# Side sums of a decoder trunk set at other ticks, w_out's sums in another stage, and a buffer of its own for raw gates

## The chip, the cores and the metric

The kernel runs on one core of a Trainium2 chip. The metric is the device time of one execution in microseconds (us). Five engines work side by side, each through its own queue in order: PE (matmuls), DVE (vector), ACT (scalar, activations), POOL (GpSimd) and SP, which here issues nearly all DMAs. A profiled execution gives a trace of every instruction.

## The reference, cut to what matters

One layer (`DEPTH = 1`), batch 1, 2048 rows of 1024 channels, all in float32:

```python
mod = silu(c) @ w_ada + b_ada
shift, scale, gate = split(mod, 3)
u = x * (1.0 + scale) + shift
h = u @ w_in
q, k, v, a_gate, p_in, p_gate, m_a, m_p = split(h)
a = sliding_window_sink_attention(q, k, v, sinks, bias, mask) * silu(a_gate)
a = a @ w_attn_proj
p = einsum('bsgc,gcd->bsgd', multiscale_causal_pool(p_in), w_pool_mix)
p = (p * pool_scale) * silu(p_gate)
p = p @ w_pool_proj
y = sigmoid(m_a) * a + sigmoid(m_p) * p
y = (y @ w_out) * (1.0 + gate)
x = layer_norm(ALPHA * x + y, ln_gain, ln_bias)
```

The attention has 16 query heads of 64 channels over 2 key heads, a window of 128, and one sink for each head. The pool means run over 2, 4, 8 and 16 rows.

## The kernel before, in words

**Products.** Each float32 operand is split into a rounded high half and a low half (`act.copy`, then the subtraction `low`), and a product takes three matmuls (`mm3`). On top of that, two output tiles by two column blocks are computed with seven block products in place of eight, from sums and differences of the blocks, as in Strassen's scheme: the weights' side is the class `Quad` (four blocks in the tile `W`, one in `A22`; `sum1`, `mid` and `late` make its sums on POOL), and the other side is seven sets, `B11`, `T1`, `T2`, `B21`, `T3`, `B22`, `T4`. A product is 12 matmuls of 128x512.

**Side sums.** The sets of one stage are made out of data of an earlier one. `sums_to` does it for one pair of row blocks: it takes two `spare` rooms, loads the four blocks (`fetch`), may multiply them (`work`), subtracts in place on POOL to get `T1`, `T2`, `T4` and `T3`, and puts each result in DRAM by SP (`put`). Its list of (offset, step) is laid over the ticks of a stage that computes something else. Four stores are filled: `u1` (the modulated x of the second half), `ain` and `pin` (attention's and pool's results, one for each half `s`), and `wo` (w_out times 1 + gate). Later a stage loads a set from its store (`set_steps`) and splits it on ACT and DVE.

**Ticks.** `ring` runs groups of two quads. After each product it calls `tick`, which emits the hooks of that place; a full group has 14 ticks. What is emitted at a tick goes to the end of its engine's queue, and `defer` holds a store back by some ticks.

**Stages.** A sequence of 2048 rows goes in two halves:

- the head, then `first_phase`: gates, keys and values of the first half, beside it the `u1` sums;
- `attention` of the first half. Its steps of scores, softmax and values are interleaved with fills, products for queries (`q`), pool inputs (`mix`) and raw gates (`ma`, `mp`). `split` prepares a fill's block three products ahead: ACT copies the high half, POOL subtracts the low half. `take_gate` copies a raw gate off PSUM into a tile and stores it; `pool_sums` and `take_p` make the pool's result in the tile `fin` (ACT copies, POOL adds, DVE scales, POOL multiplies by the gate) and store it two or three steps later (`keep_raw`);
- `second_phase`: first one group of the last gates (`post`, 14 ticks), then five groups for the second half. Beside it run the sums of `wo` (four) and of the first half's `ain` and `pin` (eight). `ph.turns["spare"]` lends rooms: two of its own pool (`None`), the four query tiles `kq`, and two of the key tile `k`, all free at that time; from group 3 on, only its own pool's four are lent;
- `attention` of the second half;
- the mix: one group of the last gates, then for each half two groups of attention projection (`attn_quad`) and two of pool projection (`pool_quad`, which adds on POOL and stores `y`), then four groups with w_out and the layer norm. Beside the first groups run the sums of the second half's `ain` and `pin`.

SP's queue holds loads and stores in one order: where a store waits for the engine that makes its data, the loads behind it wait too.

Of the kernel before, what the change touches and what calls it, by code (L numbers as in the profile page):

```python
# [12 lines left out]
F32 = mybir.dt.float32  # L13
# [6 lines left out]
P = 128  # L20
# [3 lines left out]
CH = 512  # L24
# [3 lines left out]
HD = 64  # L28
# [31 lines left out]
def kernel(  # L60
# [22 lines left out]
    nc = tc.nc  # L83
# [34 lines left out]
    wo_d = set_store("wo")  # L118
# [11 lines left out]
    def low(engine, dst, src, hi):  # L130
        engine.tensor_tensor(dst, src, as32(hi), ALU.subtract)  # L131
# [63 lines left out]
    def put(q, store, name, i, src):  # L195
        q.dma_start(store[name][i // 2, :, i % 2, :], src)

    def sums_to(ph, store, i, load, work=None):

        b = []  # L200

        def x(r, c):
            return b[r][:, c * CH : (c + 1) * CH]

        def fetch():
            b.extend((ph.spare(), ph.spare()))
            b.reverse()
            for r in (1, 0):
                load(b[r], r)

        def sub(out, a, c):
            return lambda: pool.tensor_tensor(x(*out), x(*a), x(*c), ALU.subtract)

        todo = [(0, fetch)]
        if work:
            todo += [(3, lambda: work(b[0], 0)), (3.5, lambda: work(b[1], 1))]
        todo += [(at, sub(*z)) for at, z in (
            (7.5, ((0, 1), (0, 1), (0, 0))),
            (9, ((1, 1), (1, 1), (0, 1))),
            (10.5, ((1, 0), (1, 0), (1, 1))),  # L220
            (12, ((0, 0), (1, 1), (0, 0))),
        )]
        made = ((4, "B11", (0, 0)), (5, "B21", (1, 0)), (6, "B22", (1, 1))) if work else ()
        for at, name, z in (
            *made, (8.6, "T1", (0, 1)), (10.1, "T2", (1, 1)), (11.6, "T4", (1, 0)), (13.1, "T3", (0, 0)),
        ):
            todo.append((at, lambda name=name, z=z: put(sp, store, name, i, x(*z))))
        return sorted(todo, key=lambda t: t[0])

# [500 lines left out]
    def attention(ph, s, fills, post, opened):  # L730
        tp = ph.t
# [82 lines left out]
        def take_gate(name, m, t, src, kept):  # L814
            x = src
            if not kept:
                x = tp.tile([P, CH], F32, tag="fin", bufs=2, name="raw")
                act.copy(x, src)
            later(now_n[0], lambda: sp.dma_start(gates_d[name][s, m, t], x))

# [23 lines left out]
        def split(i):  # L844
            x, name = seq[i]
            q = quads[x]
            if name == "B11" and x > 1:
                q.sum1(pool)
            w = ph.split()
            hi, lo = made[i] = w[:, 0:CH], w[:, CH:]  # L850
            act.copy(hi, q.block(name))
            low(pool, lo, q.block(name), hi)
            if name == "T1":
                q.mid(pool)
            elif name == "B21":
                q.late(pool)
# [95 lines left out]
        for n in range(N + 3):  # L952
# [11 lines left out]
            if n - 3 in pvs:  # L964
                pv = pvs.pop(n - 3)
                jj, tt, bb = (n - 3) // U, (n - 3) // NB % 2, (n - 3) % NB
                if bb == 0:
                    outs[jj, tt] = tp.tile([P, CH], F32, tag="o", bufs=2, name="o")
                if bb == 1:
                    ags[jj, tt] = ld("ag", gates_d["ag"][s, jj, tt], 1)  # L970
                o2 = tp.tile([HD, 2, P], F32, tag="o2", bufs=2, name="o2")
                dve.tensor_copy(o2, pv[HD:])
                for h in range(2):
                    dve.tensor_tensor(
                        outs[jj, tt][h * HD : (h + 1) * HD, bb * P : (bb + 1) * P], pv[0:HD, h, :], o2[:, h, :], ALU.add
                    )
# [376 lines left out]
    def second_phase(ph, opened, post, plan1):  # L1353
        groups, fills, _, turn = plan1
        cb = ph.t.tile([P, D], F32, tag="cb", bufs=1, name="cb")
        hooks = {}

        def gate_rows():
            nc.scalar.dma_start(gate_d.rearrange("k p -> p k"), mod[:, 16:24], allow_slow_non_contiguous=True)
            nc.scalar.dma_start(cb, gate_d.rearrange("k p -> (k p)").partition_broadcast(P))  # L1360

        def load_wo(x, k):
            for n in range(2):
                sp.dma_start(cols(x, n), wout[k, n])

        side = []
        for i in range(4):
            ks = (i, 4 + i)
            side.append(sums_to(
                ph,  # L1370
                wo_d,
                i,
                lambda x, r, ks=ks: load_wo(x, ks[r]),
                lambda x, r: dve.tensor_tensor(x, x, cb, ALU.mult),
            ))
        for raw in (ain_d[0], pin_d[0]):
            for i in range(4):
                side.append(sums_to(ph, raw, i, load_raw(raw, i)))
        ahead, hooks = hooks, {}
        for start, todo in zip((3, 8, 12, 16, 20, 24, 28, 32, 36, 40, 57, 62), side):  # L1380
            for offset, f in todo:
                at = int(start + offset) - 14
                if at < 0:
                    ahead.setdefault((0, at + 14), []).append(f)
                else:
                    hooks.setdefault((at // 14, at % 14), []).append(f)
        later_hooks, hooks = hooks, ahead
        hooks.setdefault((0, 2), []).append(gate_rows)
        planned(hooks, ph, u1_d, True)
        opened = ring(ph, [post], opened, hooks, groups[0], lambda tick: [front(ph, q, tick) for q in groups[0]])  # L1390
        hooks = later_hooks
        planned(hooks, ph, None, False)
        hooks.setdefault((3, 0), []).append(lambda: ph.turns.clear())
        turned(hooks, lambda i: turn(ph, i), 4)
        opened_by = [q for _, _, q in fills[:2]]
        return ring(ph, groups, opened, hooks, opened_by, lambda tick: [front(ph, opened_by[0], tick)])
# [24 lines left out]
    def cols2(t, n):  # L1421
        return t[:, n * D : (n + 1) * D]
# [18 lines left out]
        opened = attention(ph, 0, plans[0][1], plans[0][2], opened)  # L1441
    with Pools("g1", spare=4, p=2, c=5) as ph:
        kq, k, v = rooms_of("second")
        ph.turns["spare"] = cycle([None, None, *kq, cols2(k, 0), cols2(k, 1)])
        opened = second_phase(ph, opened, plans[0][2], plans[1])
    with Pools("a1") as ph:
        opened = attention(ph, 1, plans[1][1], plans[1][2], opened)
# [3 lines left out]
    with Pools("mix", spare=4, p=2, c=8) as ph:  # L1451
        for k in range(4, KT):
            ta[k] = wide(ph, k)
        phases = [([plans[1][2]], None)]
        for s in range(2):
            phases.append((pairs(lambda m, s=s: attn_quad(s, m)), ain_d[s]))
            phases.append((pairs(lambda m, s=s: pool_quad(s, m)), pin_d[s]))
        outs = [out_quad(k) for k in range(0, S // P, 2)]
        phases.append(([outs[i : i + 2] for i in range(0, 8, 2)], wo_d))
        every = [(i, gi) for i, (groups, _) in enumerate(phases) for gi in range(len(groups))]  # L1460
        sides = [{} for _ in phases]
        for n, (raw, i) in enumerate((raw, i) for raw in (ain_d[1], pin_d[1]) for i in range(4)):
            for offset, f in sums_to(ph, raw, i, load_raw(raw, i)):
                at = int(2 + 7.5 * n + offset)
                i, gi = every[at // 14]
                sides[i].setdefault((gi, at % 14), []).append(f)
        for i, (groups, store) in enumerate(phases):
            hooks = sides[i]
            if i:
                planned(hooks, ph, store, False)  # L1470
            after, nxt = None, []
            if i + 1 < len(phases):
                planned(hooks, ph, phases[i + 1][1], True)
                nxt = phases[i + 1][0][0]
                after = lambda tick, nxt=nxt: [front(ph, q, tick) for q in nxt]
            else:
                for at, row in ((1, 2), (1, 3), (5, 4), (5, 5)):
                    hooks.setdefault((0, at), []).append(lambda row=row: load_z(ph, row))
            if i in (3, 5):
                ta.clear()  # L1480
            if i == 4:

                def vectors():
                    for name, src in (("gain", gain), ("lnb", lnb)):
                        vec[name] = wide(ph, len(vec))
                        sp.dma_start(vec[name], src.partition_broadcast(P))

                hooks.setdefault((-1, 5), []).append(vectors)
                hooks.setdefault((-1, 7), []).append(lambda: [load_z(ph, row) for row in range(2)])
            opened = ring(ph, groups, opened, hooks, nxt, after, i == 5)  # L1490
# [53 lines left out]
```

## Time and profile before

| | us |
|---|---|
| median of 3 runs | 1759.96 |
| the runs | 1758.97, 1759.96, 1761.0 |
| the profiled execution, its own time | 1762.15 |
| its span in the trace | 1760.3 |

The span has 24568 instructions. In the profile, lines of code are named L and their number; most operations go through a helper that records them all at line 56, so a group is told by its tile, written out<-in. `w_set` is a pair of halves of weights, `set_B...` and `set_T...` are sets, `mm` and `lg` are PSUM banks, `spare`, `second_qs` and `second_kk` are rooms of side sums, `raw` and `fin` the tiles of the attention, `g` a gate's tile in the mix.

A row of a window gives its stretch, its length, and for PE, PE's weight loads, DVE, ACT and POOL the busy time with the number of instructions in brackets, then the granted PE clock as a share of full speed, the DMA engines' mean busy share and GB/s. A row of waits gives who waited for whom: us in total, times, longest. A row of the timeline gives start, length, engine, line, operation, tiles and count, and in square brackets the engine's idle time before it and what ended that. A row of a tile's or line's own view gives minimum, median and maximum in ns, and the first and last start. In a row of groups, the busy time and the mean in ns of one follow the first bar.

In the trace, the first attention lies from about 275 to 620 us, the second projection stage from about 630 to 860, the second attention up to about 1225, and the mix from there to the end.

### The profile page before, as it was taken

How to read it: one execution, taken by the hardware profiler on the slowest of the kernel's cores; microseconds unless marked ns; L12 is line 12 of the kernel's file. 1: busy time of each engine (PE TensorE's matmuls, PEld its weight loads, DVE VectorE, ACT ScalarE, POOL GpSimd, SP SyncE). 2: the span in 40 equal slices, each digit the busy share in tenths (PEclk: the TensorE clock that was granted, in tenths of full speed). 3: DMA queues.
4: the chain of work that ended last, by engine and by line, in shares of the span. 5: the costliest groups of instructions: out<-in, count | busy, mean ns of one | idle time of the engine just before them, and what ended most of it. 6: DMA issues, size and time to landing. Idle time of an engine off the chain costs nothing.

```text
span 1760.3 us, 24568 instructions
## 1 busy us (share of the span) xinstructions
PE 1673.0 (95%) x8056; PEld 1396.0 (79%) x8056; DVE 1219.1 (69%) x2228; ACT 964.7 (55%) x2002; POOL 1087.6 (62%) x810
## 2 busy tenths in 40 slices
PE   6899999999999997999999999989999979999997
PEld 5688888888788786788788887878877758887885
DVE  5966655787667668555477786766778476869777
ACT  4544546667567554334467676765655145534552
POOL 2154337686867836894486978597576872467442
PEclk9999999999999999999999999999999999999998
DMA  9478843333423368984432434233988786677442
GB/s 347 137 286 301 219 155 96 115 126 108 138 97 102 126 240 296 318 297 140 154 120 85 138 125 134 94 92 122 347 298 295 243 288 206 225 267 259 146 143 107
DMA packets 185840, 331.54 MB, mean 188 GB/s; under 512 B 17888, under 2 KB 43632, under 8 KB 185712
## 3 DMA queue, kind: packets, MB, share of 16 engines
q1 hardware_dynamic: 182592, 325.72, 54.4%
q10 hardware_dynamic: 3088, 4.23, 1.0%
q8 instruction: 64, 1.05, 0.2%
q14 instruction: 64, 0.52, 0.1%
q0 software_dynamic: 32, 0.02, 0.0%
HBM read 223.77 MB, written 109.28 MB: 189 GB/s over the span
## 4 chain that ended last, share of the span: by engine, by line
PE 42%; POOL 8%; DVE 7%; DMA 5%; issue 4%; ACT 3%; SPq 0%; POOLq 0%; DVEq 0%; ACTq 0%
PE mm L56 27%; PE lg L56 12%; PE pv L56 2%; DVE w_set L131 2%; PE pt L56 1%; POOL spare L56 1%; POOL w_set L56 1%; POOL wide L597 1%; DMA set_T<-ain_T 1%; DVE set_T L56 1%; POOL W L256 1%; DMA W<-in_wpp_dram 1%; POOL fin L56 1%; DMA g<-mp_d 1%; DVE set_B L56 1%
## 5 line engine op out<-in xcount | busy, mean ns | idle before, releaser
L56 PE MATMUL mm<-set_B,w_set 128*128 128x512 f32 x2664 | 665.0, 397 | 21.9 <-DVE set_B L56 9.2
L56 PEld LDWEIGHTS mm<-set_B,w_set 128*128 128x128 f32 x2664 | 501.8, 191 | 134.1 <-DVE w_set L131 11.4
L56 PE MATMUL mm<-set_T,w_set 128*128 128x512 f32 x1824 | 457.8, 397 | 7.2 <-POOL w_set L56 4.1
L56 PE MATMUL lg<-set_T,w_set 128*128 128x512 f32 x1728 | 422.6, 395 | 18.3 <-DVE w_set L131 9.2
L56 PEld LDWEIGHTS mm<-set_T,w_set 128*128 128x128 f32 x1824 | 337.3, 189 | 79.4 <-POOL w_set L56 6.3
L56 PEld LDWEIGHTS lg<-set_T,w_set 128*128 128x128 f32 x1728 | 325.6, 190 | 93.5 <-DVE w_set L131 14.5
L131 DVE TENSOR_TENSOR w_set<-W,w_set 128x1024 fp32r<-128x1024 f32 x138 | 200.0, 1451 | 193.6 <-ACT w_set L293 184.6
L293 ACT CAST w_set<-W 128x1024 fp32r<-128x1024 f32 x138 | 144.8, 1050 | 268.4 <-PE mm L56 139.5
L56 POOL TENSOR_TENSOR w_set<-W,w_set 128x512 fp32r<-128x512 f32 x160 | 208.0, 1307 | 128.1 <-ACT w_set L56 122.6
L256 POOL TENSOR_TENSOR W<-W,A 128x512 f32<-128x512 f32 x46 | 67.8, 1475 | 247.0 <-DMA A<-in_win_dram 97.6
L56 ACT ACTIVATE L<-L,nm 128x257 f32<-128x257 f32 (+1 forms) x256 | 127.1, 498 | 21.9 <-DVE nm L56 15.6
L265 POOL TENSOR_TENSOR W<-W 128x512 f32<-128x512 f32 x46 | 73.1, 1589 | 99.4 <-DVE w_set L131 88.2
L56 DVE COPY o<-pv 64x256 f32<-64x256 f32 x128 | 54.2, 424 | 104.9 <-PE pv L56 103.8
L56 DVE CUSTOM_DVE_ANT_0 L<-lg,bt,nsink 128x256 f32<-128x256 f32 (+1 forms) x256 | 111.7, 473 | 21.0 <-PE lg L56 7.5
L56 ACT CAST w_set<-W 128x512 fp32r<-128x512 f32 (+1 forms) x164 | 100.2, 626 | 39.7 <-POOL W L56 26.7
L56 POOL TENSOR_TENSOR spare<-spare 128x512 f32<-128x512 f32 x64 | 112.6, 1762 | 5.1 <-DVE spare L56 2.2
L56 ACT CAST pth<-pt 128x512 fp32r<-128x512 f32 (+1 forms) x128 | 72.8, 569 | 77.0 <-PE pt L56 76.3
L56 POOL TENSOR_TENSOR W<-W 128x512 f32<-128x512 f32 x82 | 109.8, 1352 | 4.2
L56 DVE TENSOR_TENSOR ptl<-pt,pth 128x512 fp32r<-128x512 f32 (+1 forms) x128 | 85.7, 670 | 32.5 <-ACT pth L56 32.4
L260 POOL TENSOR_TENSOR W<-W 128x512 f32<-128x512 f32 x44 | 73.4, 1672 | 40.7 <-DVE w_set L131 31.6
L261 POOL TENSOR_TENSOR W<-W 128x512 f32<-128x512 f32 x44 | 75.6, 1718 | 22.2 <-DMA W<-in_win_dram 14.3
L56 DVE TENSOR_SCALAR L<-L,sm 128x256 f32<-128x256 f32 (+1 forms) x128 | 88.9, 695 | 0.0
(227 smaller groups left out, 2423.4 us busy)
## 6 DMA issues: line engine op xcount, KB each, us to landing
W<-in_win_dram SPq DMA_DIRECT2D x42, 512.0 KB, 5.4
W<-in_win_dram SPq DMA_DIRECT2D x42, 256.0 KB, 3.9
A<-in_win_dram SPq DMA_DIRECT2D x42, 256.0 KB, 4.5
ag_d<-sig SPq DMA_DIRECT2D x32, 256.0 KB, 6.1
pg_d<-sig SPq DMA_DIRECT2D x32, 256.0 KB, 4.5
pg<-pg_d SPq DMA_DIRECT2D x32, 256.0 KB, 3.2
pin_B<-fin SPq DMA_DIRECT2D x32, 256.0 KB, 2.2
ag<-ag_d SPq DMA_DIRECT2D x32, 256.0 KB, 2.9
```

Of the source, the lines that this page charges most:

```text
L56: return lambda *args, **kw: self.tc.keep_in_program_order(op(*args, **kw))
L131: engine.tensor_tensor(dst, src, as32(hi), ALU.subtract)
L256: e.tensor_tensor(self.w[:, 1, :], self.w[:, 2, :], self.a22, ALU.add)
L260: e.tensor_tensor(x[:, 1, :], x[:, 1, :], x[:, 0, :], ALU.subtract)
L261: e.tensor_tensor(x[:, 2, :], x[:, 0, :], x[:, 2, :], ALU.subtract)
L265: e.tensor_tensor(x[:, 3, :], x[:, 3, :], x[:, 1, :], ALU.subtract)
L293: a.copy(by_two(hi), raw)
L597: nc.gpsimd.tensor_tensor(dst, g, dst, ALU.add)
```

## The change

- `sums_to` without `work`: the subtractions stand at offsets 4, 5.5, 7 and 8.5 (before 7.5, 9, 10.5, 12), their stores 2.5 ticks after each (before 1.1). With `work`, the subtractions stay at 7.5 to 12 with stores at 10 to 14.5, and the blocks stored as they are go at 5, 5.6 and 6.2 (before 4, 5, 6).
- `second_phase`: the sums of `ain` and `pin` come first, from tick 14 on and 4.5 ticks apart; w_out is loaded, multiplied and stored as four plain blocks from tick 57 on, without sums (`sums=False`), `B12` among them. The rooms are lent in another order.
- The mix: the sums of `wo` follow those of `ain` and `pin`, and all twelve start 8 ticks apart (before eight, 7.5 apart). They load the four blocks of `wo` again.
- `attention`: raw gates get the tile `raw` with one buffer (before, two of `fin`, shared with the pool's results); of `T1` the low half is made by DVE (before POOL); `o2` has one buffer (before two).
- The scratch for dynamic DMAs is 1024 (before 2048).

```diff
-    def sums_to(ph, store, i, load, work=None):
+    def sums_to(ph, store, i, load, work=None, sums=True):
...
-        todo += [(at, sub(*z)) for at, z in (
-            (7.5, ((0, 1), (0, 1), (0, 0))),
-            (9, ((1, 1), (1, 1), (0, 1))),
-            (10.5, ((1, 0), (1, 0), (1, 1))),
-            (12, ((0, 0), (1, 1), (0, 0))),
-        )]
-        made = ((4, "B11", (0, 0)), (5, "B21", (1, 0)), (6, "B22", (1, 1))) if work else ()
-        for at, name, z in (
-            *made, (8.6, "T1", (0, 1)), (10.1, "T2", (1, 1)), (11.6, "T4", (1, 0)), (13.1, "T3", (0, 0)),
-        ):
+        made = [("B11", (0, 0)), ("B21", (1, 0)), ("B22", (1, 1))] if work else []
+        if work and not sums:
+            made.insert(1, ("B12", (0, 1)))
+        puts = [(5 + 0.6 * n, *x) for n, x in enumerate(made)]
+        if sums:
+            at = 7.5 if work else 4
+            for out, a, c, name in (
+                ((0, 1), (0, 1), (0, 0), "T1"),
+                ((1, 1), (1, 1), (0, 1), "T2"),
+                ((1, 0), (1, 0), (1, 1), "T4"),
+                ((0, 0), (1, 1), (0, 0), "T3"),
+            ):
+                todo.append((at, sub(out, a, c)))
+                puts.append((at + 2.5, name, out))
+                at += 1.5
+        for at, name, z in puts:
             todo.append((at, lambda name=name, z=z: put(sp, store, name, i, x(*z))))
...
-                x = tp.tile([P, CH], F32, tag="fin", bufs=2, name="raw")
+                x = tp.tile([P, CH], F32, tag="raw", bufs=1, name="raw")
...
-            low(pool, lo, q.block(name), hi)
+            low(dve if name == "T1" else pool, lo, q.block(name), hi)
...
-                o2 = tp.tile([HD, 2, P], F32, tag="o2", bufs=2, name="o2")
+                o2 = tp.tile([HD, 2, P], F32, tag="o2", bufs=1, name="o2")
...
         side = []
+        for raw in (ain_d[0], pin_d[0]):
+            for i in range(4):
+                side.append(sums_to(ph, raw, i, load_raw(raw, i)))
...
                 lambda x, r: dve.tensor_tensor(x, x, cb, ALU.mult),
+                False,
             ))
-        for raw in (ain_d[0], pin_d[0]):
-            for i in range(4):
-                side.append(sums_to(ph, raw, i, load_raw(raw, i)))
-        for start, todo in zip((3, 8, 12, 16, 20, 24, 28, 32, 36, 40, 57, 62), side):
+        for start, todo in zip((14, 18.5, 23, 27.5, 32, 36.5, 41, 45.5, 57, 61, 65, 69), side):
...
-        ph.turns["spare"] = cycle([None, None, *kq, cols2(k, 0), cols2(k, 1)])
+        ph.turns["spare"] = cycle([cols2(k, 0), cols2(k, 1), None, None, *kq])
...
-        for n, (raw, i) in enumerate((raw, i) for raw in (ain_d[1], pin_d[1]) for i in range(4)):
+        for n, (raw, i) in enumerate((raw, i) for raw in (ain_d[1], pin_d[1], wo_d) for i in range(4)):
             for offset, f in sums_to(ph, raw, i, load_raw(raw, i)):
-                at = int(2 + 7.5 * n + offset)
+                at = int(2 + 8 * n + offset)
```

More of the change, by code (lines that the diff above doesn't have):

```diff
@@ L1374, in second_phase @@
                 lambda x, r: dve.tensor_tensor(x, x, cb, ALU.mult),
+                False,
             ))
-        for raw in (ain_d[0], pin_d[0]):
-            for i in range(4):
-                side.append(sums_to(ph, raw, i, load_raw(raw, i)))
         ahead, hooks = hooks, {}
-        for start, todo in zip((3, 8, 12, 16, 20, 24, 28, 32, 36, 40, 57, 62), side):
+        for start, todo in zip((14, 18.5, 23, 27.5, 32, 36.5, 41, 45.5, 57, 61, 65, 69), side):
             for offset, f in todo:
                 at = int(start + offset) - 14
[L1383 to L1386, printed above, removed]
+                hooks.setdefault((at // 14, at % 14), []).append(f)
         later_hooks, hooks = hooks, ahead
@@ L1531 @@
     }
-    nc = _bacc.Bacc("TRN2", target_bir_lowering=False, num_devices=1, dynamic_dma_scratch_size=2048)
+    nc = _bacc.Bacc("TRN2", target_bir_lowering=False, num_devices=1, dynamic_dma_scratch_size=1024)
     arrays, args = {}, []
```

## The prediction, made before the changed kernel ran

> **What bounds the kernel now.** I read the page's engine table first, then busy time by stretches of 50 us, then the chain of waits where a stretch does less than its neighbour.
>
> ```profile
> PE 1673.0 (95%) x8056; PEld 1396.0 (79%) x8056; DVE 1219.1 (69%) x2228; ACT 964.7 (55%) x2002; POOL 1087.6 (62%) x810
> ...
> 400.00:450.00 50.00, 50.00 (x276) 43.30 (x275) 38.39 (x111) 37.45 (x103) 35.26 (x30) 1.00 0.41 132
> 450.00:500.00 50.00, 46.17 (x234) 38.72 (x233) 28.03 (x90) 29.30 (x84) 41.27 (x34) 0.93 0.34 111
> ...
> 550.00:600.00 50.00, 46.63 (x246) 39.49 (x245) 32.68 (x94) 28.38 (x83) 47.64 (x41) 0.97 0.32 102
> ...
> 650.00:700.00 50.00, 40.80 (x165) 32.68 (x164) 37.94 (x31) 21.46 (x28) 32.84 (x17) 0.93 0.77 276
> 700.00:750.00 50.00, 47.80 (x203) 38.61 (x202) 28.54 (x29) 16.63 (x25) 38.95 (x26) 0.97 0.92 323
> 750.00:800.00 50.00, 50.00 (x222) 41.42 (x221) 25.57 (x25) 18.70 (x27) 43.52 (x29) 1.00 0.79 275
> ...
> 1050.00:1100.00 50.00, 47.49 (x259) 40.28 (x258) 35.92 (x98) 33.22 (x95) 43.59 (x36) 1.00 0.38 124
> ...
> 1150.00:1200.00 50.00, 45.74 (x243) 39.06 (x242) 32.95 (x91) 29.56 (x84) 47.79 (x40) 0.97 0.33 105
> ...
> 1400.00:1450.00 50.00, 37.63 (x139) 27.91 (x138) 33.30 (x29) 18.85 (x22) 34.18 (x20) 0.90 0.87 300
> ```
>
> PE is the bound, at 95%, but busy time hides lost work, because overlapping matmuls count twice. The number in brackets says more. In attention a full stretch holds 276 matmuls (0.181 us each), in the projection stages 222 (0.225 us each). Against these the stretches lose: 450 to 500, 42 x 0.181 = 7.6 us; 550 to 600, 30, so 5.4; 1050 to 1100, 17, so 3.1; 1150 to 1200, 33, so 6.0: **22.1 us in the two attentions**. 650 to 700 loses 57 x 0.225 = 12.8 and 700 to 750 loses 19, so 4.3: **17.1 us in the second projection stage**. 1400 to 1450 loses 83, so **18.7 us in the mix**. Those 58 us are all that this change can address; the rest of the idle time lies in the head and at the stage borders. Why is each lost?
>
> The attention's losses, by the list of waits and the chain that ended last (start, duration, what):
>
> ```profile
> ACT raw L56 <- DMA pin_B<-fin: 31.9, 5, 9.3
> ...
> 1178.87 1.27 POOL fin L56
> ...
> 1180.16 2.21 DMA pin_B<-fin
> ...
> 1182.47 0.59 ACT raw L56
> ...
> 1184.84 0.48 ACT pth L56
> ...
> 1186.09 0.73 PE pv L56 x3
> ```
>
> The copy of a raw gate takes a `fin` buffer, so ACT stands until POOL has finished a pool result and its store has landed. Behind it on ACT wait the softmax and `pth`, and PE waits for `pth`. Five such waits hold 31.9 us, the longest 9.3. After each, PE restarts at a lower granted clock (0.93 in 450 to 500).
>
> The mix's loss, by SP's own waits from 1380 to 1460, DMA share in 2 us slices of the same window, and the timeline:
>
> ```profile
> SPq L56 <- POOL spare L56: 26.6, 5, 9.8
> ...
> DMA  9900019999999999999999379999600389999949
> ...
> 1395.71 4.06 SPq L56 DMA_DIRECT2D g<-mp_d  x6
> ...
> 1402.04 0.69 DVE L595 TENSOR_TENSOR g<-mm,g 128x512 f32<-128x512 f32 x1 [5.76 <-DMA g<-mp_d]
> ```
>
> SP's queue is in order. It holds the store of a side sum that POOL has not made, the DMA engines stand idle (the slices 0001), and the gate loads behind it come late; then everything is asked for at once and the DMA engines are full for 30 us.
>
> The second projection stage, by the timeline:
>
> ```profile
> 670.80 4.53 DVE L56 TENSOR_TENSOR second_qs<-second_qs,cb 128x1024 f32<-128x1024 f32 x2
> ...
> 677.59 2.71 PE L56 MATMUL mm<-set_B,w_set 128*128 128x512 f32 x6 [4.49 <-DVE set_B L56]
> ...
> 690.49 2.35 DVE L56 TENSOR_TENSOR second_qs<-second_qs,cb 128x1024 f32<-128x1024 f32 x2
> ...
> 695.09 4.29 PE L56 MATMUL mm<-set_B,w_set 128*128 128x512 f32 x11 [4.71 <-DVE set_B L56]
> ```
>
> DVE multiplies w_out by the gate in front of the set's low halves, and PE waits 4.49 and 4.71 us for those.
>
> **The change part by part.** *Raw copies in their own place.* The five waits on `pin_B` go. What is late next? POOL: from 550 to 600 it is busy 47.64 us while PE does 246 of 276, so at full rate it would need 47.64 x 276 / 246 = 53.4.
>
> ```profile
> L56 POOL TENSOR_TENSOR w_set<-W,w_set 128x512 fp32r<-128x512 f32 x160 | 208.0, 1307 | 128.1 <-ACT w_set L56 122.6 <-PE mm L56 5.4
> ...
> L131 DVE TENSOR_TENSOR w_set<-A,w_set x48: 676/689/1781, 81.0 to 1743.7; 128x512 fp32r<-128x512 f32 x48
> ...
> L56 POOL TENSOR_TENSOR spare<-spare x64: 1278/1734/2299, 89.5 to 1439.7; 128x512 f32<-128x512 f32 x64
> ...
> 400.02 0.38 SPq L56 DMA_DIRECT2D ma_d<-raw  x1
> ...
> 401.25 0.59 ACT L56 COPY raw<-mm 128x512 f32<-128x512 f32 x1 [0.16 <-DMA pin_B<-fin]
> ...
> DMA to landing us min/median/max: 2.0/2.4/5.2
> ```
>
> *T1's low half from POOL to DVE.* There are 14 in each attention, about two in 50 us, so POOL sheds 2 x 1.307 = 2.6 us and needs 50.8: about 0.9 us still lost in each of the two fullest stretches, 1.8 in all. On DVE the nearest row (same shape, both inputs in SBUF) has 0.689 us in the median and 1.781 at most. From 400 to 450, at full rate, DVE is busy 38.39 of 50; two halves add 1.4 to 3.6. So they fit. POOL's `mid` now waits for DVE's half, and all that is queued on POOL with it; what `mid` makes is split one product later. In DVE's queue the softmax of the next step stands behind a half that waits for ACT's copy. The cost lies between nothing and 28 x 0.689 = 19.3 us if every one ends on PE's path; a gain is counted in POOL's relief already. I take 2, near nothing, because of DVE's free time.
>
> Here a rule speaks against the change. POOL's 128x512 takes 1.278 at least and 2.299 at most, DVE's half 0.676 and 1.781: both stretch by about 1 us in places. The Trainium skill, "SBUF — State Buffer", section "Who interferes with whom", says that a VectorE instruction with two SBUF inputs and a GpSimd instruction that reads SBUF exclude each other for the whole instruction. The stretched rows agree. By that rule POOL would be held 0.689 for each half and shed half as much, which leaves some 2.8 us more in the two fullest stretches: 1728 in place of the 1725 below.
>
> *One buffer for raw, in place of two shared.* A store lands 2.4 us after its issue in the median. The copy at 401.25 comes 1.2 us after the issue of the store before it and would wait some 1.5 us more; of the second attention I expect the same. Both ends: nothing, and 5.2 us a time at the longest landing. I take 2. Attention: 22.1 - 1.8 - 2 - 2 = **16 us gained**. The second buffer of `o2` goes too, at nothing: DVE both writes and reads it, in order.
>
> *Second projection stage.* No side work stands in its first 14 ticks any more, and the eight multiplies come at ticks 60 to 72, where DVE has 25.57 of 50 busy (750 to 800) as cover; without that cover they would cost again the two waits, 9.2 us. The attention's and pool's sums then start right at tick 14, at one pair of inputs in 4.5 ticks (before: 4), so POOL and the DMA engines (share 0.92 from 700 to 750) stay loaded there, though 16 subtractions and 16 stores fewer pass their queues in this stage, and four stores of a raw block more. Of 17.1 I take the two DVE waits and a little of what followed them, **11 us**; the bounds are 3 and 15.
>
> *The mix.* A tick is 12 matmuls:
>
> ```profile
> 702.11 2.72 PE mm L56 x12
> ...
> L56 SPq DMA_DIRECT2D spare<-pin_B x28: 320/432/882, 747.8 to 1394.2; - x28
> ...
> spare<-pin_B SPq DMA_DIRECT2D x4, 256.0 KB, 4.6
> ...
> 1308.00:1350.00 42.00, 40.40 (x177) 32.83 (x176) 29.90 (x29) 23.91 (x31) 23.80 (x15) 1.00 1.01 368
> ...
> 1446.00:1484.00 38.00, 37.08 (x164) 30.36 (x163) 27.30 (x26) 20.92 (x31) 16.05 (x11) 1.00 0.70 234
> 1484.00:1523.00 39.00, 39.00 (x174) 32.30 (x173) 30.81 (x29) 19.95 (x25) 12.80 (x8) 1.00 0.83 287
> ```
>
> A store now follows its sum by 2.5 ticks, 6.8 us, in place of 1.1 ticks, 3.0. Five waits of 26.6 us are 5.3 each; 3.8 us less on each leaves 1.5. The slices 0001 go, most of the burst with them. POOL's lag stays, so I take 12 of the 18.7. In return w_out's sums stand at ticks 66 to 101 (about 1430 to 1525, by the count of matmuls): 16 more loads and 16 stores of 256 KB, 8.4 MB over 95 us, 88 GB/s on top of 234 and 287. That brings this stage to the load that 1308 to 1350 has (368 GB/s, share 1.01), where 177 matmuls stand for 42 / 0.225 = 187, a loss of 2.2 in 42 us. POOL gets 16 subtractions of 1.734 us, 27.7 us over 95, and has room at 16.05 of 38. I take 4 for it all. Mix: **8 us gained**; the bounds are a loss of 6 and a gain of 19. The first stage's later stores meet a PE that waits for none of them; nothing.
>
> Sum: 16 + 11 + 8 = 35. The profiled execution took 1762.15 us (span 1760.3 and 1.85 around it), 2.2 above the median of 1759.96. 1762.15 - 35 - 2.2 = **1725 us**.
>
> **Rivals.** (a) *Turned into DMA time.* For it: shares of 0.92 and 1.01 in the stretches where sums are made, and 5.2 MB that nobody moved before (16 reloads, 4 stores). Against: the waits begin with idle DMA engines. Then the mix gains nothing and the second projection 5: 1762.15 - 21 - 2.2 = 1739.
>
> (b) *DVE takes POOL's place in the attention.* For it: DVE is the fullest engine behind PE there. Against: it has 11.6 us free in 50. Every half on the path costs 19.3 in place of 2: the gain is 18, so 1742.
>
> (c) *Slower: POOL waits for the side loads.* A sum now stands 4 ticks behind its fetch, 10.9 us, where it was 7.5 ticks, 20.4. Four issues at 0.432 and a landing of 4.6 take 6.3, so 4.6 us are left. Once SP is later than that, POOL stands in front of the sums for W, ACT and PE behind it. For it: the gate loads at 1395.71 came so late that DVE stood 5.76 us. Against: that lag came from the very waits that shrink. Should the last 7 of the mix's 12 sums each pass on 5 us, 35 are lost, with (a)'s gain of 21 left: 1774.
>
> **How the numbers follow.** My forecast has 0.62, (a) 0.17, (b) 0.10, (c) 0.08, and 0.03 stays for what I don't see. The low end takes every part at its best, 22 + 15 + 19 = 56: 1704. The high end takes attention at 6, between forecast and (b), the second projection at 3, and the mix at a loss of 6: a gain of 3, 1757. Only (c) and part of the rest lie beyond. A measurement can tell about 0.2%, 3.5 us, from no change. Faster by more than that: forecast, (a), (b) nearly whole, 0.88; same 0.03; slower 0.09.
>
> **What would show it.** Right: no ACT `raw` wait on `pin_B`, and 450 to 500 with about 270 matmuls; no PE wait on `set_B` near 677 and 695; SP's waits on `spare` in the mix halved, and the stretch of 139 near 190. (a): DMA shares of 1.0 around a mix that still loses 15 us. (b): PE idle behind DVE in attention. (c): POOL `spare` released by DMA, for more than 10 us in all. Wrong: the attention's counts unchanged though `raw` waits for nothing.

## The result, and the profile after

| | us |
|---|---|
| before, median of 4 runs beside it | 1760.48 (1758.97 to 1762.35) |
| changed, median of 4 runs | 1734.40 (1732.64 to 1737.16) |
| ratio | 0.9853, 95% interval 0.9836 to 0.987 |
| changed, the profiled execution (span) | 1734.67 (1732.9) |

The change gains 26.1 us, 1.5%. Where they come from is read off the score matmuls of the two attentions, `lg<-kk,qs`, 256 in each: the stage borders below are their first and last starts. The rows of `qs` give them for a whole run (columns: count, duration in ns, first and last start); the inner borders come from the same row in a window of one attention. First before, then after:

```profile
L56 PE MATMUL lg<-kk,qs x512: 220/280/419, 271.4 to 1213.9; 128*128 128x256 f32 x160, 128*128 128x128 f32 x11
L56 PE MATMUL lg<-kk,qs x256: 220/280/419, 271.4 to 613.9; 128*128 128x256 f32 x112, 128*128 128x128 f32 x16
L56 PE MATMUL lg<-kk,qs x256: 277/280/416, 873.5 to 1213.9; 128*128 128x256 f32 x128
```

```profile
L56 PE MATMUL lg<-kk,qs x512: 220/280/355, 270.4 to 1181.1; 128*128 128x256 f32 x160, 128*128 128x128 f32 x11
L56 PE MATMUL lg<-kk,qs x256: 220/280/286, 270.4 to 602.1; 128*128 128x256 f32 x112, 128*128 128x128 f32 x16
L56 PE MATMUL lg<-kk,qs x256: 277/280/355, 848.5 to 1181.1; 128*128 128x256 f32 x128
```

| us | head and first projection | attention 1 | second projection | attention 2 | mix |
|---|---|---|---|---|---|
| before | 271.4 | 342.5 | 259.6 | 340.4 | 546.4 |
| changed | 270.4 | 331.7 | 246.4 | 332.6 | 551.7 |
| difference | -1.0 | -10.8 | -13.2 | -7.8 | **+5.3** |
| predicted | 0 | -16 in both | -11 | | **-8** |

The attentions gave 18.6 and the second projection 13.2; the mix took 5.3 back. Each length comes from one profiled execution, and is good to 0.1 us as a reading. As a measurement it is coarser: in ten kernels of this document whose attentions have the code of the changed one, the two attentions together take 661.6 to 666.6 us, and in three kernels with the same mix the mix takes 551.7 to 553.1. Differences of 2 or 3 us between two profiles are not far above that spread.

The engines over the whole span and the stretches of the changed kernel, in the columns of before:

```profile
PE 1665.9 (96%) x8056; PEld 1392.2 (80%) x8056; DVE 1257.8 (73%) x2256; ACT 964.5 (56%) x2002; POOL 1063.0 (61%) x782
```

```profile
450.00:500.00 50.00, 49.80 (x268) 41.95 (x268) 36.59 (x102) 33.34 (x94) 43.60 (x36) 1.00 0.44 142
550.00:600.00 50.00, 47.57 (x257) 40.10 (x256) 39.35 (x100) 33.04 (x95) 46.33 (x38) 1.00 0.37 121
...
650.00:700.00 50.00, 50.00 (x222) 41.43 (x221) 37.61 (x31) 23.56 (x33) 38.13 (x23) 1.00 0.78 277
700.00:750.00 50.00, 50.00 (x222) 41.39 (x221) 25.09 (x26) 17.45 (x25) 41.07 (x28) 1.00 0.78 266
750.00:800.00 50.00, 48.07 (x212) 39.49 (x211) 37.26 (x36) 22.70 (x35) 22.26 (x15) 1.00 0.60 207
...
1125.00:1175.00 50.00, 48.26 (x262) 40.91 (x261) 40.33 (x101) 32.45 (x91) 48.82 (x39) 1.00 0.34 111
...
1350.00:1400.00 50.00, 42.20 (x167) 33.02 (x166) 27.47 (x25) 15.64 (x19) 36.56 (x24) 0.90 0.85 304
1400.00:1450.00 50.00, 46.88 (x193) 37.62 (x193) 38.06 (x31) 22.47 (x30) 43.08 (x25) 0.93 0.76 261
```

450 to 500 went from 234 matmuls to 268 of 276; 550 to 600, where POOL is fullest, only from 246 to 257, and the same place in the second attention (1150 to 1200 before, 1125 to 1175 now) from 243 to 262; 650 to 750 went from 368 to a full 444; 750 to 800, where DVE now multiplies w_out, pays 10. But 1350 to 1450 holds 360 of 444, a loss of 84 x 0.225 = 18.9 us: the hole that before had at 1400 to 1450 (18.7) is still there, only earlier, as the stage starts 33 us sooner. Counted in pieces of 60 us from the start of the stage, the hole lies between 180 and 240 us and holds 184 matmuls, before 183. What the mix lost lies elsewhere: up to 420 us it does 23 matmuls fewer than before, 5.2 us, 9 of them in the first 60 us and 11 between 360 and 420.

SP's waits in the mix (counted from 1180 to 1735, before's two rows are the same from 1214 to the end; us, times, longest), before and then after:

```profile
SPq L56 <- POOL spare L56: 54.6, 15, 9.8
SPq L56 <- POOL wide L597: 47.2, 16, 14.6
```

```profile
SPq L56 <- POOL wide L603: 61.1, 24, 7.5
SPq L56 <- POOL spare L56: 60.5, 20, 6.5
```

The mean wait for a side sum fell from 3.6 us to 3.0, not to 1.5. Beside it stands a second row of the same queue, which the prediction never looked at: the stores of `y` (`y_d<-wide`), which wait for POOL's additions in `pool_quad`. Those rose from 47.2 to 61.1. In the hole alone, before (1380 to 1460) the side sums held SP 26.6 us, as the prediction's row has it, and `y` only 1.0; now (1340 to 1420) the two share it:

```profile
SPq L56 <- POOL wide L597: 1.0, 2, 0.7
```

```profile
SPq L56 <- POOL wide L603: 13.4, 7, 4.4
SPq L56 <- POOL spare L56: 12.2, 5, 4.6
```

The hole in the timeline of the changed kernel, and in windows of 10 us:

```profile
1359.07 5.22 SPq L56 DMA_DIRECT2D y_d<-wide  x2
...
1364.35 3.84 SPq L56 DMA_DIRECT2D g<-mp_d  x8
...
1375.11 1.04 ACT L56 CAST set_B<-set_B 128x1024 fp32r<-128x1024 f32 x1 [8.39 <-DMA set_B<-ain_B]
...
1378.50 1.22 PE L56 MATMUL lg<-set_T,w_set 128*128 128x512 f32 x2 [5.68 <-ACT w_set L299]
```

```profile
1350.00:1360.00 10.00, 10.00 (x45) 8.26 (x44) 2.32 (x2) 2.99 (x5) 10.00 (x8) 1.00 0.49 161
1360.00:1370.00 10.00, 8.66 (x37) 6.40 (x36) 1.97 (x3) 1.53 (x2) 9.92 (x8) 1.00 0.59 187
1370.00:1380.00 10.00, 4.04 (x15) 2.51 (x13) 3.34 (x3) 4.59 (x5) 2.40 (x2) 0.82 1.04 385
```

SP stands in front of two `y` stores; the eight gate loads and the set's loads behind them go out late; ACT waits 8.39 us for a set, its cast of `w_set` waits behind that, and PE 5.68 us for the cast. The DMA engines are about half busy first (0.49 and 0.59), then full (1.04) when all that SP held is asked for at once. The chain of waits that leads there, from 1340 to 1368, shows what SP stands behind: POOL with one instruction after the other.

```profile
1355.30 1.25 POOL spare L56
1356.54 1.25 POOL W L266
1357.79 1.26 POOL wide L603
1359.05 2.24 POOL spare L56
...
1361.37 1.29 POOL spare L56
1362.66 1.25 POOL wide L603
1363.91 1.26 POOL W L266
...
1367.81 5.32 DMA g<-mp_d
```

### The profile page after: what moved, and what is told of

Same layout as the page of the kernel before. It is cut to its first block, busy times and chain, and to the rows that moved or that the text cites. A ratio compares the mean times of both kernels' runs of the same rounds, so it can differ in the third digit from the quotient of the medians.

```text
span 1732.9 us, 24692 instructions
## 1 busy us (share of the span) xinstructions
PE 1665.9 (96%) x8056; PEld 1392.2 (80%) x8056; DVE 1257.8 (73%) x2256; ACT 964.5 (56%) x2002; POOL 1063.0 (61%) x782
## 3 DMA queue, kind: packets, MB, share of 16 engines
HBM read 227.96 MB, written 110.33 MB: 195 GB/s over the span
## 4 chain that ended last, share of the span: by engine, by line
PE 44%; POOL 7%; DVE 6%; DMA 5%; issue 4%; ACT 2%; SPq 1%; POOLq 0%; DVEq 0%; ACTq 0%
PE mm L56 28%; PE lg L56 12%; PE pv L56 2%; POOL wide L603 2%; PE pt L56 2%; DVE w_set L131 2%; POOL spare L56 1%; POOL W L262 1%; SPq L56 1%; DVE set_T L56 1%; ACT w_set L299 1%; DMA W<-in_wap_dram 1%; DMA g<-ma_d 1%; POOL W L266 1%; POOL w_set L56 1%
## 5 line engine op out<-in xcount | busy, mean ns | idle before, releaser
L131 DVE TENSOR_TENSOR w_set<-W,w_set 128x1024 fp32r<-128x1024 f32 x138 | 207.9, 1507 | 173.9 <-ACT w_set L299 164.0
L56 POOL TENSOR_TENSOR w_set<-W,w_set 128x512 fp32r<-128x512 f32 x132 | 171.9, 1310 | 101.2 <-ACT w_set L56 91.3
L262 POOL TENSOR_TENSOR W<-W,A 128x512 f32<-128x512 f32 x46 | 71.5, 1554 | 218.1 <-DMA A<-in_win_dram 75.5
L56 POOL TENSOR_TENSOR spare<-spare 128x512 f32<-128x512 f32 x68 | 121.0, 1782 | 13.0 <-DMA spare<-ain_B 9.1
L56 ACT ACTIVATE L<-L,sm 128x256 f32<-128x256 f32 (+1 forms) x128 | 64.3, 503 | 68.1 <-DVE sm L56 67.8
L56 DVE TENSOR_SCALAR L<-L,sm 128x256 f32<-128x256 f32 (+1 forms) x128 | 89.9, 702 | 0.0
```

The lines of the kernel that those rows point to most:

```text
L56: return lambda *args, **kw: self.tc.keep_in_program_order(op(*args, **kw))
L262: e.tensor_tensor(self.w[:, 1, :], self.w[:, 2, :], self.a22, ALU.add)
```

## The experiments

All edits are on the changed kernel unless said. Theory: the raw gate's own buffer made the attentions' gain and w_out's move the second projection's; in the mix SP's queue is held by whatever POOL is late with, the stores of `y` as well as those of the side sums. Rivals: T1's halves on DVE carry the attentions; w_out's sums alone cost the mix; the sums' nearer loads do. Ratios are to the kernel before, on the same chip (the changed kernel: 0.9853); stage lengths are from each one's profiled execution, as above.

**The raw gates back in `fin`.**

```diff
-                x = tp.tile([P, CH], F32, tag="raw", bufs=1, name="raw")
+                x = tp.tile([P, CH], F32, tag="fin", bufs=2, name="raw")
```

> The changed kernel (1734.4 us) with raw gates' copies back in the two fin buffers that they shared with pool results; all else as changed. Theory (the raw copy behind a pool result's store was what held the attentions): the waits of ACT raw on pin_B<-fin come back, over 20 us in all, and the time is 10 to 18 us more, 1744 to 1752. Rival (POOL's relief by the T1 halves is what shortened the attentions): those waits stay under 10 us and the time is under 1739.

1749.25 us, ratio 0.992 (0.99 to 0.9939). The attentions take 341.2 and 338.4, 15.3 more than in the changed kernel (by the two ratios the whole kernel is 11.8 longer); the second projection 245.9, as there. The wait of before is back:

```profile
ACT raw L56 <- DMA pin_B<-fin: 35.1, 6, 8.1
```

**The same edit the other way, on the kernel before:** only `raw` in its own buffer (and one buffer of `o2`, and the smaller scratch, to make room).

```diff
-                x = tp.tile([P, CH], F32, tag="fin", bufs=2, name="raw")
+                x = tp.tile([P, CH], F32, tag="raw", bufs=1, name="raw")
```

> The kernel before with one part of the change alone: raw gates' copies in one buffer of their own (o2 with one buffer and the smaller scratch make the room). Theory: the two attentions lose 13 to 17 us and nothing else moves: a ratio to the kernel before of 0.990 to 0.993. Rival (the parts need each other, POOL being late next without the T1 halves on DVE): 3 to 9 us, 0.995 to 0.998.

1749.60 us, ratio 0.9923 (0.9908 to 0.9938); attentions 333.0 and 335.9, 14.0 less than before. Taken away it costs 15.3, added alone it gives 14.0 (13.6 by the ratio): the gain of the buffer needs neither T1's halves nor the moved sums.

**T1's low half back on POOL.**

```diff
-            low(dve if name == "T1" else pool, lo, q.block(name), hi)
+            low(pool, lo, q.block(name), hi)
```

> The changed kernel with the low half of T1 back on POOL in the attentions; all else as changed. Theory (the raw copy does it, the halves do little): within 4 us of 1734.4. Rival (POOL is what is late next, so its relief by 28 x 1.3 us counts): 5 to 12 us more, with the loss in the last third of each attention where POOL is fullest. Second rival (DVE is the cost): 2 to 6 us less.

1737.38 us, ratio 0.9852 (0.9835 to 0.9869), the changed kernel's. In its profile the attentions are 3.7 longer (333.1 and 334.9), about 1.5 beyond the spread given above, and PE waits 4.2 us for POOL's halves (1.2 in the changed kernel); in the ratio nothing shows. What the halves do on DVE is seen in POOL's queue, in the changed kernel; with the halves on POOL neither row is there:

```profile
POOL W L56 <- DVE sm L56: 30.3, 12, 3.9
POOL W L56 <- DVE w_set L56: 19.2, 10, 3.7
```

POOL's `mid` now stands 49.5 us for DVE, as feared, and it costs PE nothing that can be measured.

**w_out's sums back in the second projection**, at the ticks and with the order of rooms of before, and only eight sums in the mix.

```diff
-        for start, todo in zip((14, 18.5, 23, 27.5, 32, 36.5, 41, 45.5, 57, 61, 65, 69), side):
+        for start, todo in zip((3, 8, 12, 16, 20, 24, 28, 32, 36, 40, 57, 62), side):
...
-        for n, (raw, i) in enumerate((raw, i) for raw in (ain_d[1], pin_d[1], wo_d) for i in range(4)):
+        for n, (raw, i) in enumerate((raw, i) for raw in (ain_d[1], pin_d[1]) for i in range(4)):
```

> The changed kernel with w_out's sums back in the second projection stage at the ticks and in the order of before, and only the eight sums of ain and pin in the mix, 8 ticks apart. Theory: the second projection stage is 10 to 13 us longer again (PE behind DVE near its 40th us), and the mix 3 to 6 us shorter, as the 16 reloads and 16 sums are gone: 1738 to 1743. Rival (the mix is bound by POOL's backlog in the pool groups, which w_out's sums don't touch): the mix stays within 2 us of the changed kernel's, so 1744 to 1748.

1743.58 us, ratio 0.989 (0.9872 to 0.9908). The second projection takes 261.4, 15.0 more, and PE's wait is back:

```profile
PE mm L56 <- DVE set_B L56: 7.5, 2, 4.5
```

```profile
650.00:700.00 50.00, 41.92 (x167) 33.08 (x166) 44.26 (x33) 20.12 (x27) 37.08 (x20) 0.93 0.90 336
```

The mix takes 548.7, 3.0 less. So w_out's sums cost the mix about 3 us, and with the new offsets alone it still isn't shorter than before (546.4).

**The offsets of before in the mix**: sums 7.5 ticks after the fetch, stores 1.1 ticks after their sum. Both go back together: counted from the fetch, the first store of before comes at 8.6 ticks, the new one, though it follows its sum by more, already at 6.5.

```diff
-            for offset, f in sums_to(ph, raw, i, load_raw(raw, i)):
+            for offset, f in sums_to(ph, raw, i, load_raw(raw, i), first=7.5, gap=1.1):
```

> Changed kernel, but the mix's side sums keep the offsets of the kernel before: first sum 7.5 ticks after its fetch, each store 1.1 ticks behind its sum (changed kernel: 4 and 2.5). Spacing (8 ticks) and w_out's sums stay. Theory (what bounds the mix's SP queue is how far POOL is behind, and a store that follows later only hands the wait on to the next y store): the mix within 3 us of the changed kernel's 551.7, ratio 0.983 to 0.987. Rival 1 (the prediction's step: a later store is worth 12 us here, and it is w_out's sums that took more than 4 back): mix at 560 to 565, ratio 0.990 to 0.993. Rival 2 (the sum standing 4 ticks behind its fetch instead of 7.5 makes POOL wait for side loads and costs more than the later store gives): mix at 545 or less, ratio below 0.982.

1730.47 us, ratio 0.9809 (0.9792 to 0.9825). The mix takes 549.0, 2.7 less than with the new offsets. The length is where the theory had it, but the ratio is where the second rival had it (below 0.982): that a sum so near its fetch makes POOL wait for side loads. So the new offsets are worth nothing in the mix; they cost some 3 us by the profiles and up to 8 by the ratios. SP's waits in its mix:

```profile
SPq L56 <- POOL spare L56: 89.0, 25, 9.2
SPq L56 <- POOL wide L603: 42.5, 19, 7.5
```

The new offsets did take SP's wait for the sums from 89.0 to 60.5, 28.5 us; 18.6 of them came back as a wait for `y`, and PE had nothing of the rest. Rival (c), the second rival here, accounts for most of the 2.7: in the changed kernel POOL waits for a side load at the start of the mix, and PE does 270 matmuls from 1180 to 1240, with the old offsets 279, 9 x 0.225 = 2.0 us.

```profile
1210.55 1.98 POOL L56 TENSOR_TENSOR spare<-spare 128x512 f32<-128x512 f32 x1 [8.68 <-DMA spare<-ain_B]
```

No such wait stands in the mix of the kernel with the old offsets. The other profiles say the same. In the kernels with raw back in `fin`, T1 on POOL, w_out's sums back, later `y` stores and spacing 6, which all have the new offsets on POOL, it is there with 8.0 to 8.6 us, and the first 60 us of the mix hold 260 or 261 matmuls at a granted clock of 0.97 (before: 276, at 1.00), 3.4 us fewer. With the sums on DVE they hold 279.

**`y`'s stores later**, held back by `defer` for 6 ticks instead of 3. POOL's work stays as it is.

```diff
-            defer(3, lambda: sp.dma_start(to, dst.rearrange("p (s q) -> p s q", s=4)))
+            defer(6, lambda: sp.dma_start(to, dst.rearrange("p (s q) -> p s q", s=4)))
```

> The changed kernel with the mix's stores of y held back 6 ticks in place of 3; all else as changed. SP waits there for POOL's additions to wide as much as for its side sums. Theory (SP's order: whatever store it holds for POOL delays the gate and set loads): SP's waits on wide fall to a third, the gate loads near 1364 us come 4 to 9 us earlier, and the mix is 5 to 10 us shorter than the changed kernel's 551.7. Rival (POOL itself is late, and PE waits for its sums of W whatever SP does): the mix stays within 3 us.

1724.12 us, ratio 0.9778 (0.9759 to 0.9796); mix 543.4, 8.3 less. SP's waits in the mix, and the loads and PE at the hole:

```profile
SPq L56 <- POOL spare L56: 67.3, 18, 9.6
SPq L56 <- POOL wide L603: 15.1, 10, 4.1
```

```profile
1356.14 5.46 SPq L56 DMA_DIRECT2D g<-mp_d  x8
...
1371.26 0.73 PE L56 MATMUL lg<-set_T,w_set 128*128 128x512 f32 x2 [1.09 <-ACT w_set L299]
```

The gate loads go out 8.2 us earlier (4.8 counted from the start of the stage, which came 3.4 sooner), and PE's wait falls from 5.68 to 1.09. No engine has less to do here: these 8.3 us come with SP's order alone. Not all of them lie in the hole: up to 420 us after its start the mix does 35 matmuls more than the changed kernel's, 23 in the hole and 27 between 360 and 420, and 15 fewer elsewhere; what the order does at that second place wasn't taken apart. Nor does SP wait less in the hole: from 1336.6 to 1416.6, the same place in the stage, it is held 31.3 us by sums and 1.0 by `y`, where the changed kernel has 12.2 and 13.4, and ahead of the gate loads 16.8 us in place of 15.3. So the sum of the waits doesn't explain the gain; what is shown is that another order of the same work gives it.

**The mix's 48 side subtractions on DVE**, and, in a kernel of its own, **the 32 additions to `wide` on DVE**.

```diff
-            return lambda: pool.tensor_tensor(x(*out), x(*a), x(*c), ALU.subtract)
+            return lambda: (eng or pool).tensor_tensor(x(*out), x(*a), x(*c), ALU.subtract)
...
-            for offset, f in sums_to(ph, raw, i, load_raw(raw, i)):
+            for offset, f in sums_to(ph, raw, i, load_raw(raw, i), eng=dve):
```

```diff
-            nc.gpsimd.tensor_tensor(dst, g, dst, ALU.add)
+            nc.vector.tensor_tensor(dst, g, dst, ALU.add)
```

> The changed kernel with the mix's 48 side subtractions on DVE in place of POOL; all else as changed. Theory (POOL is late in the mix, SP holds its stores for it, and the gate and set loads behind them come late): the stall near 1372 us shrinks, SP's waits on the sums fall under 25 us, and the mix is 8 to 16 us shorter: 1718 to 1727. Rival (the mix is bound by the bytes that the DMA engines move there): the DMA share stays full around the set's change and the time stays within 4 us of 1734.4. Rival (DVE takes POOL's place): slower, 1738 or more.

> The changed kernel with the 32 additions to wide in the pool groups on DVE in place of POOL; side sums stay on POOL. Theory (POOL's sum of work in the pool groups is what is late, no matter which part): about what the sums on DVE gave, 8 to 16 us shorter than the changed kernel. Rival (it is the side sums' place in POOL's queue that matters): within 4 us of the changed kernel.

Sums on DVE: 1717.19 us, ratio 0.9733 (0.9714 to 0.9753), mix 535.0, 16.7 less. Additions on DVE: 1722.18 us, ratio 0.9766 (0.975 to 0.9783), mix 539.3, 12.4 less. Both take work off POOL, so that its sums for `W` come earlier too; how much of their gain is SP's and how much is ACT and PE waiting for `W` wasn't taken apart. With the sums on DVE, SP's waits in the mix are

```profile
SPq L56 <- POOL wide L603: 66.4, 26, 8.5
SPq L56 <- DVE spare L56: 18.5, 13, 4.0
```

The wait for `y` hasn't become less although POOL is busy 221 us in place of 296 from 1200 to 1650.

**The mix's sums 6 ticks apart, w_out's from tick 72.**

```diff
-                at = int(2 + 8 * n + offset)
+                at = int((2 + 6 * n if n < 8 else 24 + 6 * n) + offset)
```

> The changed kernel with the mix's first eight side sums 6 ticks apart in place of 8, so that only two of them fall into the pool groups, where POOL also adds to wide, and w_out's four from tick 72 on; all else as changed. Theory (POOL is late in the pool groups because side sums come on top of wide): the stall near 1372 us shrinks by half or more and the mix is 6 to 12 us shorter than 551.7. Rival (DMA: the first groups have a share of 0.85 to 0.95 already): the loss moves ahead of 1330 us and the mix stays within 3 us, or grows.

1728.04 us, ratio 0.9802 (0.9787 to 0.9816); mix 545.7, 6.0 less. SP waits 35.5 us for sums, in place of 60.5, and 57.5 for `y`.

**Two and three of these together.**

> Changed kernel, mix's 48 side subtractions on DVE and the y stores deferred by 6 calls instead of 3. Theory (two sorts of stores held SP: the side sums' and y's, both behind POOL; with the sums gone from POOL, y's stores wait less already): most of the gain of the sums on DVE alone (16.7 us in the mix) and a third of the 8.3 of the later y stores: mix at 530 to 534, ratio 0.970 to 0.973. Rival (the two gains add): mix at 527, ratio 0.968. Rival (they are the same gain): mix at 535, ratio 0.9733.

> Changed kernel, y stores deferred by 6 calls and the mix's sums 6 ticks apart (w_out's from tick 72), everything else on POOL as it is. Alone they gave 8.3 and 6.0 us in the mix. Theory (each removes SP's wait behind POOL in another place: the spacing where a sum meets POOL's own group, the deferral where y's result is late): mix at 540 to 542, ratio 0.976 to 0.977. Rival (they add): mix at 537, ratio 0.972 to 0.974.

> Changed kernel, mix's 48 side subtractions on DVE, y stores deferred by 6 calls, sums 6 ticks apart with w_out's from tick 72. Theory (with POOL early nothing is left for the spacing to remove): as the kernel with the sums on DVE and the later y stores, mix at 530 to 534, ratio 0.970 to 0.973. Rival (the spacing also thins the loads, 368 GB/s at the start of the mix, and adds its own 6 us): mix at 526, ratio 0.967 to 0.969.

| kernel | us | ratio | mix |
|---|---|---|---|
| sums on DVE, `y` later | 1706.08 | 0.9675 (0.9658 to 0.9692) | 525.5 |
| `y` later, spacing 6 | 1722.15 | 0.9759 (0.9745 to 0.9774) | 540.9 |
| all three | 1711.74 | 0.9705 (0.9688 to 0.9721) | 530.0 |

My theory was wrong for the first: the two gains add (16.7 + 8.3 = 25.0; measured 26.2). They take away different waits:

```profile
SPq L56 <- DVE spare L56: 28.1, 18, 4.9
...
SPq L56 <- POOL wide L603: 15.1, 12, 4.0
```

```profile
1343.66 4.56 SPq L56 DMA_DIRECT2D g<-mp_d  x8
```

The gate loads go out 20.7 us earlier than in the changed kernel (19.0 counted from the start of the stage). Between 1300 and 1420 one PE wait of over 1 us is left, 3.63 us at 1383; the changed kernel has three, of 1.15, 5.68 and 3.08. The spacing gives 2.5 us with `y` later and costs 4.5 with both: my reading, which no run shows, is that it was a way round POOL's load, and without that load only sets things closer. The first of the three is the fastest kernel of this study, 28 us below the changed one by the times and 31 by the ratios.

## Why the prediction was right, and where it wasn't

Forecast 1725, measured 1734.4: inside 1704 to 1757 and faster, as the likeliest case said. By profiled executions 1762.15 - 1734.67 = 27.5 us were gained of 35, and the stages close on that: 18.6 + 13.2 + 1.0 - 5.3. The total is nearer than its parts: the mix came out 13.3 below its price, the attentions and the second projection together 4.8 above theirs. In that the number is partly luck.

- *Raw copies in their own place.* Right, and the largest term: 14.0 and 15.3 us by the profiles of two experiments, 13.6 and 11.8 by their ratios. ACT's waits on `pin_B` for `raw` are gone. POOL was late next, as said, but by more: the two stretches where POOL is fullest, 550 to 600 and 1125 to 1175, still lose 19 and 14 matmuls, 6.0 us where I had 1.8. That the attentions gave 18.6 and not less than 16 comes from the 4 us set aside for T1's halves and the single buffer, which weren't needed: two errors that about cancel. And "after each, PE restarts at a lower granted clock" was too wide: before, it does after the waits of 7.77, 9.32 and 8.53 us (0.66 from 470 to 480, 0.83 from 575 to 585 and from 1180 to 1190), but after the one of 6.09 the clock is 1.00 (1070 to 1080).
- *T1's halves.* Priced at a cost of 2, they cost nothing measurable; the attentions of the profile are 3.7 shorter with them. POOL does wait for DVE (49.5 us), but PE isn't behind that. For the Trainium skill's rule in "SBUF — State Buffer", section "Who interferes with whom" (a VectorE instruction with two SBUF inputs and a GpSimd instruction that reads SBUF exclude each other), I had 2.8 us more lost in those two stretches, and 4.2 more were; but with the halves back on POOL the same stretches hold 248 and 255 matmuls in place of 257 and 262, so no run shows that the rule is the reason.
- *One buffer for raw.* Priced at 2; the copies wait 1.0 us in all for their own stores (one wait). Nothing.
- *Second projection.* 13.2 against 11. No PE wait on `set_B` is left; putting the sums back brings two of them, 7.5 us, and 15.0 us in the stage. The multiplies at ticks 60 to 72 are not quite covered: the ten matmuls missing from 750 to 800 are 2.3 us.
- *The mix: the step that failed.* I took back 12 of the 18.7 us because each store follows its sum 3.8 us later, and 4 off for w_out's sums. The second was about right: 3.0. The first gave none: the hole stayed as it was (184 matmuls after 183), and with the old offsets the mix is 2.7 shorter. 2.7 + 3.0 = 5.7 would account for the 5.3 measured, if the two add, which no run shows. The step reckoned that what SP no longer waits for a sum is time won for the loads behind it. But POOL's work stayed, and the stores of `y` wait for the same engine: in the hole before, the sums held SP 26.6 us and `y` 1.0; in the hole now, 12.2 and 13.4, together 25.6 after 27.6. In the whole mix the stores of `y` had held SP 47.2 us already before, nearly as much as the sums' 54.6, most of it (44.3) after 1460, outside the window that the prediction was priced from. The sum, set nearer to its fetch, had its price besides, POOL's wait for a side load at the start of the mix, which I had only as rival (c). What the store's 3.8 us alone would have given is open, as no run moves the store without the sum.
- *What would show it.* "SP's waits on `spare` in the mix halved, and the stretch of 139 near 190" failed, and pointed at the right step: 60.5 after 54.6, and 167 at the hole.
- *Rivals.* (a) had the mix at no gain, but for DMA time, and its sign did come: from 1370 to 1410, around PE's waits of 5.68 and 3.08, the DMA share is 1.01 to 1.07. But the bytes come bunched: just ahead of that the share is 0.49 and 0.59. And a later place for `y`'s stores took 8.3 us out of the stage with the same bytes moved (227.96 MB read and 110.33 written in both). How long PE would wait without the burst wasn't tested. (b) didn't come. (c) came with one wait of 8.7 us for `ain_B` and one of 1.6 for `pin_B` in the mix, worth 2.0 us here, 3.4 in sister kernels, not 35.

## What to carry to other kernels

In a queue that runs in order, list every sort of store that waits for the same late engine, over the whole stage, before pricing one of them: here setting the side sums earlier and their stores further behind them gave nothing, delaying the other stores 8.3 us, and taking the sums off the late engine 16.7. A buffer that two producers of different pace share can be worth a second one: here one more tile was the largest part of the change. And time that a queue waits isn't time lost: with the new offsets SP waited 10 us less for POOL in the mix, and the mix was 2.7 us longer.

## What was not expected of the hardware

The same subtraction of 128x512 took half the time on DVE as on POOL. Mean ns in the mix, the changed kernel and the one with the sums on DVE:

```profile
L56 POOL TENSOR_TENSOR spare<-spare 128x512 f32<-128x512 f32 x48 | 89.9, 1876 | 11.1 <-DMA spare<-ain_B 8.7 <-DMA spare<-pin_B 1.6
L603 POOL TENSOR_TENSOR wide<-g,wide 128x512 f32<-128x512 f32 x32 | 58.4, 1832 | 34.7 <-DVE g L601 34.7
```

```profile
L603 POOL TENSOR_TENSOR wide<-g,wide 128x512 f32<-128x512 f32 x32 | 61.3, 1924 | 39.2 <-DVE g L601 39.2
...
L56 DVE TENSOR_TENSOR spare<-spare 128x512 f32<-128x512 f32 x48 | 44.3, 923 | 0.1
```

48 of them cost POOL 89.9 us and DVE 44.3. POOL's own additions became no shorter with 75 us less to do, but a little longer, 1924 ns in place of 1832, as DVE's load beside them grew from 338 us to 371 between 1200 and 1650; that has the sign which the rule of "SBUF — State Buffer", section "Who interferes with whom", in the Trainium skill would give it, but no run takes the rule apart from other causes. DVE, the fullest engine behind PE in the stage, had the room all the same.
